# Attention scores whose two products both span 128 partitions, decay ranks with one stationary shape, and later starts for some steps

## The chip, the cores and the metric

The kernel runs on one core of one Trainium2 chip. A core has a matrix engine (TensorE, "PE" in the profile, with its weight loads shown as "PEld"), VectorE ("DVE"), ScalarE ("ACT"), GpSimd ("POOL") and SyncE ("SP"), which here only issues DMA transfers. Each engine works through its own queue in order. The metric is the device time of one execution in microseconds, the median of the runs.

## The reference, cut to what matters

One layer of an encoder on 1024 tokens of width 1024: a half-step feed-forward block with a norm, a mixer with a norm, another half-step feed-forward block with a norm. The mixer projects once, runs neighbourhood attention (8 heads of 64, a window of 8 x 16 on a 16 x 64 grid) and gated linear attention (GLA) in two directions, gates both, and projects out. All in float32.

```python
x <- LN1(alpha*x + 0.5*SwiGLU_1(x))
x <- LN2(alpha*x + W_out(sig(g_na)*P_na(NA(x)) + sig(g_gla)*P_gla(GLA(x))))
x <- LN3(alpha*x + 0.5*SwiGLU_2(x))
# NA, for one row of queries
scores = einsum('bhqd,bhiqjd->bhqij', q_r, k_sel) + bias
p = softmax(scores)
out = einsum('bhqij,bhiqjd->bhqd', p, v_sel)
# GLA, decay of one direction: the decay ranks dec_lr are 16 columns of the projection
log_a = log_sigmoid(dec_lr @ w_dec2 + b_dec) / 16
```

## The kernel before, in words

**Precision.** Matmuls run on a rounded float32 type. A number x is split into a high part xh (x rounded) and a low part xl = x - xh, and a product is the sum of three matmuls: high by high, high by low, low by high. Most filler of PE is such triples of a 128x128 stationary block with 512 moving columns (lines L122 to L124, L559 to L561, L659 to L661, L871 to L873). One triple is one *filler step*; the code counts it as STEP = 0.65 units of its own clock.

**Order.** PE's order is written out by hand. `run` walks through streams of filler steps, adds each step's cost to the clock, and after every step emits the actions whose due time has passed; `at(delay, fn)` queues an action. So an action falls on the first step at or past its due time. The other engines' orders are made by a scheduler from program order and priority.

**Neighbourhood attention.** There are 64 units: 4 head pairs, 2 halves of the rows, 4 blocks of columns, 2 heads. Unit i has, one unit time apart, `na_scores(i)` (two matmuls into one PSUM tile s; then DVE adds the bias and finds the maximum, ACT the exponential, DVE the division), two units later `na_transpose(i)` (three transposes on PE, a copy on ACT), and three units later `na_values` (for two heads at a time, 12 small matmuls). NA_T0 is the due time of unit 0 and NA_DT the distance of units. Filler between them is a projection of V for the GLA (`tok_major`, L871 to L873) and four gates (`gate_gla`, L122 to L124), together 83.2 units of the clock.

**Score operands.** For a pair of heads p, `qk_pair` loads from DRAM, on POOL's queue: for each head the tile q2, which has the high part of that head's q on its own 64 partitions and the low part on the other 64; the tile k2, which has the high part of k on both halves; and one tile kl with the low parts of k of both heads, 64 partitions each. The first score product is q2 by k2 over 128 partitions, (qh + ql) by kh. The second is qh by kl, over the 64 partitions of that head only. `v_block` loads a column block of V for the pair on SP's queue, into a quarter of one tile vp per pair. For pairs 1 to 3, POOL first writes a mark into each new tile, from the small tile of the latest score unit, which holds the loads back to that point.

**Decay ranks.** `decay_rank` multiplies x by 32 columns. Its stationary block of 64 columns has the high part of the weights in columns 0 to 31 and the low part in 32 to 63. By the high part of x all 64 columns are used (L971), by the low part only the first 32 (L967, L970); the two halves of the 64 output rows are added at the end. There are 2 x 16 matmuls of 512 columns.

**Norms.** `Norm` collects eight tiles of 128 features. Its steps are due by lags after each other: lags[0] from the fourth tile to `shift` (L237: a matmul with ones, which gives a provisional mean), lags[1] from the last centring to `stats` (L269: transposes of the sums, then small DVE work), lags[2] to `scale` and lags[3] to `scale2` (L302: matmuls that spread the scales), after which `apply` runs over the eight tiles (two DVE operations, two on ACT, and the low part xl on POOL, L412). LAGS_B is for the second half of the tokens in the first norm, LAGS_2B for the same half in the second norm. The work behind them that needs their result: the fifth token block of `tok_major` (L871 to L873), and the second half of the first gate of the last feed-forward block (L122 to L124).

Of the kernel before, what the change touches and what calls it, by code (L numbers as in the profile page):

```python
# [8 lines left out]
F32 = mybir.dt.float32  # L9
F32R = mybir.dt.float32r  # L10
# [8 lines left out]
P = 128  # L19
D = 1024  # L20
S = 1024
KD = D // P
# [18 lines left out]
GLA_DT = 31.0  # L41
GLA_NEXT = 8.5
GLA_OUT = (15.0, 28.8, 28.8, 35.5)
NA_T0 = 18.0
NA_DT = 0.97
NA_GATES = (4, 5, 6, 7)
GLA_GATES = (1, 2, 3)
FIRST = (1, 2, 4, 8)
STEP = 0.65
LAGS_A = (5.0, 9.5, 8.0, 2.0)  # L50
GAP_A = 1.0
LAGS_B = (2.6, 5.5, 4.7, 1.3)
LAGS_3A = (5.0, 8.0, 9.2, 1.7)
LAGS_3B = (5.0, 7.0, 5.7, 0.2)
GAP_3A = 2.0
GAP_3B = 0.5
LAGS_2A = (7.3, 8.4, 5.6, 2.0)
LAGS_2B = (2.7, 6.1, 3.9, 1.0)
LN_POOL = (1, 2, 3, 5)

COL0 = (0, 8, 24, 40)
COLW = (24, 32, 32, 24)
# [5 lines left out]
def hybrid_layer(ctx, tc, xT, wg1, wu1, wds1, wd1, wg2, wu2, wds2, wd2, wcol, wnv, wgv, wdl, wgate,  # L68
                 wbr, wout, lnp, bias, dec2, bdec, ng, ident_d, masks_d, ln3, outN):
    nc = tc.nc  # L70

    ln_lags = {(0, 0): (LAGS_A, GAP_A), (0, 1): (LAGS_B, 0.0),
               (2, 0): (LAGS_3A, GAP_3A), (2, 1): (LAGS_3B, GAP_3B)}
# [21 lines left out]
    def nm(s):  # L95
        uid[0] += 1
        return f"{s}_{uid[0]}"
# [29 lines left out]
    def dps(shape=(P, HF)):  # L127
        return dense.tile(list(shape), F32, tag="d", name=nm("d"))

    def split(src, hi, lo):  # L130
        nc.scalar.activation(hi, src, AF.Copy)  # L131
        nc.vector.tensor_tensor(lo, src, hi.bitcast(F32), ALU.subtract)  # L132
# [29 lines left out]
    for c1 in FIRST:  # L162
        w = slice(c0 * P, c1 * P)
# [20 lines left out]
    def at(delay, fn):  # L184
        uid[0] += 1
        pending.append((clock[0] + delay, uid[0], fn))
        pending.sort(key=lambda e: e[:2])
# [237 lines left out]
    def stage():  # L425
        return lp.tile([P, HF], F32, tag="sl", name=nm("sl"), bufs=2)
# [391 lines left out]
    x1 = [[None, None] for _ in range(KD)]  # L818
# [22 lines left out]
    qks = dram.tile([4, 4, P, S], F32, tag="qks", name="qks")  # L841
# [114 lines left out]
    def decay_rank():  # L956
        raw = wpool.tile([P, KD, 32], F32, tag="raw", name=nm("raw"), bufs=2)
        nc.sync.dma_start(raw, wdl)
        w = wpool.tile([P, KD, 64], F32R, tag="wh", name=nm("wh"))
        nc.scalar.activation(w[:, :, 0:32], raw, AF.Copy)  # L960
        nc.vector.tensor_tensor(w[:, :, 32:64], raw, w[:, :, 0:32].bitcast(F32), ALU.subtract)
        for h in range(2):
            ps = dps((64, HF))
            for k in range(KD):
                xh, xl = x1[k][h]
                if k:
                    nc.tensor.matmul(ps[0:32], w[:, k - 1, 0:32], x1[k - 1][h][1], start=False,  # L967
                                     stop=False)
                if k == KD - 1:
                    nc.tensor.matmul(ps[0:32], w[:, k, 0:32], xl, start=False, stop=False)  # L970
                nc.tensor.matmul(ps, w[:, k], xh, start=k == 0, stop=k == KD - 1)  # L971
                yield STEP * 2 / 3
            sb = stage()
            nc.scalar.activation(sb[0:32], ps[32:64], AF.Copy)
            nc.vector.tensor_tensor(sb[0:32], sb[0:32], ps[0:32], ALU.add)
            hi, lo = one.tmp(), one.tmp()
            split(sb[0:32], hi[0:32].bitcast(F32R), lo[0:32].bitcast(F32R))
            for i, t in enumerate((hi, lo, hi)):
                nc.sync.dma_start(dls[32 * i:32 * i + 32, h * HF:(h + 1) * HF], t[0:32])
# [18 lines left out]
    npool = pool(nap, "npool")  # L998
    o_na = [[None, None] for _ in range(4)]
    grid = lambda t: t.rearrange("p (r c) -> p r c", c=64)  # L1000
    pair = {}

    def qk_pair(p, mark=None):
        k2 = [npool.tile([P, S], F32R, tag="k2", name=nm("k2"), bufs=4) for _ in range(2)]
        kl = npool.tile([P, S], F32R, tag="kl", name=nm("kl"), bufs=2)
        vp = npool.tile([P, 16, P], F32, tag="vp", name=nm("vp"), bufs=2)
        q2 = [[None, None], [None, None]]
        pair[p] = (q2, k2, kl, vp)
        load = lambda dst, src: nc.gpsimd.dma_start(dst.bitcast(F32), src)
        for h in range(2):  # L1010
            for hh in range(2):
                q2[hh][h] = npool.tile([P, HF], F32R, tag="q2", name=nm("q2"), bufs=8)
        if mark is not None:
            m = mark[:, 0:1]
            for t in (*k2, kl, *q2[0], *q2[1]):
                nc.gpsimd.tensor_copy(t[:, 0:1], m)
        for h in range(2):
            hs = slice(h * HF, (h + 1) * HF)
            for hh in range(2):
                a, o = slice(64 * hh, 64 * hh + 64), slice(64 - 64 * hh, 128 - 64 * hh)  # L1020
                t = q2[hh][h]
                load(t[a], qks[p, 0, a, hs])
                load(t[o], qks[p, 1, a, hs])
                if h == 0:
                    load(k2[hh][a], qks[p, 2, a])
                    load(k2[hh][o], qks[p, 2, a])
            if h == 0:
                load(kl, qks[p, 3])

    def v_block(p, b, mark=None):  # L1030
        vp, w = pair[p][3], COLW[b]
        if mark is not None:
            nc.gpsimd.tensor_copy(vp[:, 4 * b:4 * b + 4, 0:1],
                                  mark[:, 0:1].unsqueeze(2).to_broadcast([P, 4, 1]))
        for g in range(4):
            nc.sync.dma_start(vp[:4 * w, 4 * b + g, :],
                              vgrid[4 * g:4 * g + 4, COL0[b]:COL0[b] + w, p * P:(p + 1) * P])


    na_e, na_t, na_b, na_o, na_mark = {}, {}, {}, {}, {}  # L1040
# [11 lines left out]

    def na_scores(i):
        p, rb, hh, b = na_idx(i)
        q2, k2, kl, vp = pair[p]
        w, c0 = COLW[b], COL0[b]
        nk = 12 * w
        if hh == 0 and b != 2:
            na_b[0] = na_b.pop("next")
            if i < 62:  # L1060
                bias_tile(i + (2 if b != 1 else 4))
        bt = na_b[0]
        a = slice(64 * hh, 64 * hh + 64)
        ka = (slice(4 * rb, 4 * rb + 12), slice(c0, c0 + w))
        qa = slice(P * b, P * b + P)
        s = aux.tile([P, 384], F32, tag="s", name=nm("s"), bufs=2)
        nc.tensor.matmul(s[:, :nk], q2[hh][rb][:, qa], grid(k2[hh])[:, ka[0], ka[1]],
                         start=True, stop=False)
        nc.tensor.matmul(s[:, :nk], q2[hh][rb][a, qa], grid(kl)[a, ka[0], ka[1]],  # L1069
                         start=False, stop=True)  # L1070
        e = npool.tile([P, 384], F32, tag="e", name=nm("e"), bufs=3)
        sm = npool.tile([P, 4], F32, tag="sm", name=nm("sm"), bufs=4)
        nc.vector.tensor_tensor_reduce(e[:, :nk], s[:, :nk], bt[:, hh, :nk], -1.0,
                                       3.0e38, ALU.add, ALU.min, sm[:, 0:1])
        nc.scalar.activation(e[:, :nk], e[:, :nk], AF.Exp, bias=sm[:, 0:1], scale=-1.0,
                             accum_out=sm[:, 1:2])
        nc.vector.reciprocal(sm[:, 2:3], sm[:, 1:2])
        nc.vector.tensor_scalar(e[:, :nk], e[:, :nk], sm[:, 2:3], None, ALU.mult)
        na_e[i] = e
        na_mark[0] = sm  # L1080
# [12 lines left out]
    def na_values(i):  # L1093
        if i % 2 == 0:
            return
        p, rb, hh, b = na_idx(i)
        vp = pair[p][3]
        if i % 8 == 1:
            na_o[0] = aux.tile([P, HF], F32, tag="o", name=nm("po"), bufs=1)
        po = na_o[0]  # L1100
        et = [na_t.pop(i - 1), na_t.pop(i)]
        w = COLW[b]
        for g in range(3):
            for hh in range(2):
                nc.tensor.matmul(po[64 * hh:64 * hh + 64, b * P:(b + 1) * P],  # L1105
                                 vp[:4 * w, 4 * b + rb + g, 64 * hh:64 * hh + 64],
                                 et[hh][:4 * w, g * P:(g + 1) * P], start=g == 0, stop=g == 2)
        if i % 8 == 7:
            hi, lo = atile(F32R), atile(F32R)
            split(po, hi, lo)  # L1110
            o_na[p][rb] = (unblk(hi), unblk(lo))
# [25 lines left out]
    for p in range(1, 4):  # L1137
        t0 = NA_T0 + (16 * p - 10.5) * NA_DT
        at(t0, lambda p=p: qk_pair(p, na_mark[0]))
        for b in range(4):  # L1140
            at(t0 + (1 + 2 * b) * NA_DT, lambda p=p, b=b: v_block(p, b, na_mark[0]))
    na_events(0, 67, NA_T0, NA_T0 + 67 * NA_DT)
    run(tok_major(wgv, lambda t: gv[t], wq=wq), *[gate_gla(j) for j in NA_GATES])
    flush()
# [189 lines left out]
    for hd in range(4):  # L1334
        b = GLA_T0 + GLA_DT * hd
# [70 lines left out]
    for h in range(2):  # L1406
        ln = Norm(HF, 1, LN_EPS, sums, tmp, to_x2(h), LAGS_2B if h else LAGS_2A,
                  0.0 if h else 2.0)
# [102 lines left out]
```

## Time and profile before

| | |
|---|---|
| median of 3 runs | 2116.47 us (2112.81 to 2116.59) |
| the profiled execution | 2112.51 us, of which 2110.7 us span |
| granted clock of PE, mean | 0.995 of full speed |
| instructions in the span | 26717 |
| neighbourhood attention, first score to last values | about 894 to 1072 us |
| decay ranks | 713 to 721 us |
| first norm, second half | statistics at 672 us |
| second norm, second half | shift at 1414 us, statistics at 1442 us |

A row of the timeline has the start and length in us, the engine, the line, the operation, the tiles written and read, the shape (for PE: rows times columns of the array that are used, then partitions times moving columns), the count, and in brackets the idle time before it with what ended it. Lengths of PE's matmuls include the way through the array, so neighbours overlap; the distance of two starts is their pace. A row of a group has busy time and mean ns behind the first bar, idle time behind the second. The table of waits has the total, the number and the longest.

### The profile page before, as it was taken

To read this page: it belongs to the slowest core of one execution; us is meant where nothing else is said; L and a number is where in the kernel's file an instruction comes from. 1 tells how busy PE (TensorE), PEld (TensorE's weight loads), DVE (VectorE), ACT (ScalarE), POOL (GpSimd) and SP (SyncE) were. 2 spreads that over 40 slices of the span, in tenths; PEclk is the share of its full clock that TensorE was granted. 3 is DMA by queue.
4 is the path that set the end of the run, shared out by engine and by line. 5 is a ranking of instruction groups with operands and counts; after the bars stand their busy time and mean duration, and the time that the engine had idled before them with its cause. 6 is when DMAs were issued, how large, how long until landed. Compare 5 with 4: busy or idle time off the path is not lost.

```text
span 2110.7 us, 26717 instructions
## 1 busy us (share of the span) xinstructions
PE 2073.1 (98%) x9722; PEld 1688.4 (80%) x9722; DVE 1379.8 (65%) x2356; ACT 898.4 (43%) x1503; POOL 163.0 (8%) x237
## 2 busy tenths in 40 slices
PE   9999999999999999989999999999999999999997
PEld 7888888888887788766678888877888888888887
DVE  8666776457668964135457774799776776457647
ACT  6444444312234644245565553445544454312222
POOL 0000000000014221212110000034000000000001
PEclk9999999999999999999999999999999999999999
DMA  4444443396630244556444334521343444396622
GB/s 143 148 150 150 158 158 124 130 330 216 221 113 30 88 170 140 153 146 184 147 123 121 110 112 143 176 89 60 118 171 127 175 143 138 122 317 217 240 99 81
DMA packets 156372, 315.59 MB, mean 150 GB/s; under 512 B 17360, under 2 KB 41680, under 8 KB 156240
## 3 DMA queue, kind: packets, MB, share of 16 engines
q1 hardware_dynamic: 136976, 268.26, 37.5%
q0 software_dynamic: 9152, 29.37, 4.7%
q10 hardware_dynamic: 10112, 16.26, 2.5%
q8 instruction: 77, 1.26, 0.2%
q14 instruction: 55, 0.45, 0.1%
HBM read 216.43 MB, written 97.39 MB: 149 GB/s over the span
## 4 chain that ended last, share of the span: by engine, by line
PE 80%; issue 7%; DVE 7%; DMA 3%; ACT 2%; POOL 2%; SPq 0%; ACTq 0%; DVEq 0%; POOLq 0%
PE d L559 16%; PE d L561 16%; PE d L560 16%; PE d L122 5%; PE d L123 5%; PE d L124 5%; PE d L659 3%; PE d L661 3%; PE d L660 3%; PE pt L1087 1%; PE po L1105 1%; PE s L1069 1%; DMA sb<-gts 1%; DMA bt<-in_bias 1%; PE d L871 1%
## 5 line engine op out<-in xcount | busy, mean ns | idle before, releaser
L131 ACT ACTIVATE wh<-raw 128x512 fp32r<-128x512 f32 (+4 forms) x148 | 111.6, 763 | 192.4 <-PE d L560 90.4
L132 DVE TENSOR_TENSOR wl<-raw,wh 128x512 fp32r<-128x512 f32 (+4 forms) x148 | 125.2, 854 | 100.9 <-ACT wh L131 100.9
L122 PE MATMUL d<-xh,wh 128*128 128x512 f32 x384 | 158.4, 413 | 1.0 <-ACT xh L131 0.9
L681 DVE TENSOR_TENSOR a<-a,d 128x512 f32<-128x512 f32 (+1 forms) x152 | 99.9, 657 | 90.9 <-PE d L561 60.5
L559 PE MATMUL d<-a,wh 128*128 128x512 f32 x384 | 149.8, 390 | 2.4 <-DVE hr L587 1.6
L123 PE MATMUL d<-xl,wh 128*128 128x512 f32 x384 | 150.9, 393 | 1.0 <-POOL xl L412 0.5
L124 PE MATMUL d<-xh,wl 128*128 128x512 f32 x384 | 151.1, 394 | 0.0
L561 PE MATMUL d<-xh,wl 128*128 128x512 f32 x384 | 149.5, 389 | 0.5 <-DVE wl L132 0.5
L559 PE MATMUL d<-hh,hh 128*128 128x512 f32 x384 | 149.5, 389 | 0.4 <-ACT hr L923 0.4
L560 PE MATMUL d<-a,wh 128*128 128x512 f32 x384 | 149.4, 389 | 0.0
L559 PE MATMUL d<-xh,wh 128*128 128x512 f32 x384 | 149.4, 389 | 0.0
L560 PE MATMUL d<-xl,wh 128*128 128x512 f32 x384 | 149.4, 389 | 0.0
L561 PE MATMUL d<-a,wl 128*128 128x512 f32 x384 | 149.4, 389 | 0.0
L560 PE MATMUL d<-hl,hh 128*128 128x512 f32 x384 | 149.4, 389 | 0.0
L561 PE MATMUL d<-hh,hl 128*128 128x512 f32 x384 | 149.4, 389 | 0.0
L131 ACT ACTIVATE hh<-sr 128x512 fp32r<-128x512 f32 x168 | 105.6, 631 | 83.7 <-PE d L560 24.4
L659 PE MATMUL d<-hh,wh 128*128 128x512 f32 (+1 forms) x368 | 134.3, 365 | 0.0
L661 PE MATMUL d<-hh,wl 128*128 128x512 f32 (+1 forms) x368 | 133.0, 362 | 0.0
L660 PE MATMUL d<-hl,wh 128*128 128x512 f32 (+1 forms) x368 | 133.0, 361 | 0.0
L132 DVE TENSOR_TENSOR hl<-sr,hh 128x512 fp32r<-128x512 f32 x168 | 114.2, 694 | 1.4 <-ACT hh L131 0.7
L111 ACT ACTIVATE wh<-raw 128x512 fp32r<-128x512 f32 (+1 forms) x77 | 67.5, 877 | 103.6 <-PE d L123 36.9
L131 ACT ACTIVATE oh<-hr 128x512 fp32r<-128x512 f32 x88 | 55.4, 631 | 131.0 <-DVE hr L588 49.0
(335 smaller groups left out, 4928.1 us busy)
## 6 DMA issues: line engine op xcount, KB each, us to landing
raw<-in_wu SPq DMA_DIRECT2D x44, 512.0 KB
raw<-in_wg SPq DMA_DIRECT2D x43, 512.0 KB
ops<-oh SPq DMA_DIRECT2D x84, 256.0 KB
ops<-ol SPq DMA_DIRECT2D x84, 256.0 KB
oh<-ops SPq DMA_DIRECT2D x48, 256.0 KB
ol<-ops SPq DMA_DIRECT2D x48, 256.0 KB
hid<-oh SPq DMA_DIRECT2D x40, 256.0 KB
hid<-ol SPq DMA_DIRECT2D x40, 256.0 KB
```

What stands on the lines that cost most here:

```text
L122: nc.tensor.matmul(ps, a, xh, start=k == 0, stop=False)
L123: nc.tensor.matmul(ps, a, xl, start=False, stop=False)
L124: nc.tensor.matmul(ps, wl[:, k * m:(k + 1) * m], xh, start=False, stop=k == n - 1)
L131: nc.scalar.activation(hi, src, AF.Copy)
L132: nc.vector.tensor_tensor(lo, src, hi.bitcast(F32), ALU.subtract)
L559: nc.tensor.matmul(ps, a, xh, start=first and k == 0, stop=False, **sg)
L560: nc.tensor.matmul(ps, a, xl, start=False, stop=False, **sg)
L561: nc.tensor.matmul(ps, wl[:, k * P:(k + 1) * P], xh, start=False, stop=k == n - 1, **sg)
L659: nc.tensor.matmul(ps, wh, hi, start=k == 0, stop=False)
L660: nc.tensor.matmul(ps, wh, lo, start=False, stop=False)
L661: nc.tensor.matmul(ps, wl, hi, start=False, stop=k == n - 1)
L681: nc.vector.tensor_tensor(a, a, ps, ALU.add)
```

## The change

- The low parts of k get a tile per head, with the same 64 rows on both halves of the partitions, as k2 has them. The second score product is then q2 by kl over all 128 partitions; it also adds the low part of q by the low part of k, which was left out. Each pair has 16 loads on POOL's queue in place of 13, and 8 marks on q and k tiles in place of 7.
- Each column block of V has a tile of its own, from 6 buffers, in place of a quarter of a tile of 2 buffers; blocks 2 and 3 are loaded 9.5 and 11.5 units after the pair's loading is due, in place of 5 and 7.
- Units of attention start at 22.0 in place of 18.0 and stand 0.91 apart in place of 0.97, so that the 67 steps end at 82.97 in place of 82.99.
- In the decay ranks all matmuls use the whole stationary block of 64 columns. Their number stays 16 per half.
- LAGS_B[1] goes from 5.5 to 7.7, LAGS_2B[0] from 2.7 to 5.2 and LAGS_2B[1] from 6.1 to 8.0.

```diff
-NA_T0 = 18.0
-NA_DT = 0.97
+NA_T0 = 22.0
+NA_DT = 0.91
...
-LAGS_B = (2.6, 5.5, 4.7, 1.3)
+LAGS_B = (2.6, 7.7, 4.7, 1.3)
...
-LAGS_2B = (2.7, 6.1, 3.9, 1.0)
+LAGS_2B = (5.2, 8.0, 3.9, 1.0)
...
                 if k:
-                    nc.tensor.matmul(ps[0:32], w[:, k - 1, 0:32], x1[k - 1][h][1], start=False,
-                                     stop=False)
+                    nc.tensor.matmul(ps, w[:, k - 1], x1[k - 1][h][1], start=False, stop=False)
+                nc.tensor.matmul(ps, w[:, k], xh, start=k == 0, stop=False)
                 if k == KD - 1:
-                    nc.tensor.matmul(ps[0:32], w[:, k, 0:32], xl, start=False, stop=False)
-                nc.tensor.matmul(ps, w[:, k], xh, start=k == 0, stop=k == KD - 1)
+                    nc.tensor.matmul(ps, w[:, k], xl, start=False, stop=True)
...
-        kl = npool.tile([P, S], F32R, tag="kl", name=nm("kl"), bufs=2)
-        vp = npool.tile([P, 16, P], F32, tag="vp", name=nm("vp"), bufs=2)
+        kl = [npool.tile([P, S], F32R, tag="kl", name=nm("kl"), bufs=4) for _ in range(2)]
...
-            for t in (*k2, kl, *q2[0], *q2[1]):
+            for t in (*k2, *kl, *q2[0], *q2[1]):
                 nc.gpsimd.tensor_copy(t[:, 0:1], m)
...
                 if h == 0:
-                    load(k2[hh][a], qks[p, 2, a])
-                    load(k2[hh][o], qks[p, 2, a])
-            if h == 0:
-                load(kl, qks[p, 3])
+                    for k, t in ((2, k2[hh]), (3, kl[hh])):
+                        load(t[a], qks[p, k, a])
+                        load(t[o], qks[p, k, a])
...
+        vp = pair[p][3][b] = npool.tile([P, 4, P], F32, tag="vp", name=nm("vp"), bufs=6)
...
-        nc.tensor.matmul(s[:, :nk], q2[hh][rb][a, qa], grid(kl)[a, ka[0], ka[1]],
+        nc.tensor.matmul(s[:, :nk], q2[hh][rb][:, qa], grid(kl[hh])[:, ka[0], ka[1]],
                          start=False, stop=True)
...
-            at(t0 + (1 + 2 * b) * NA_DT, lambda p=p, b=b: v_block(p, b, na_mark[0]))
+            at(t0 + (1, 3, 9.5, 11.5)[b] * NA_DT, lambda p=p, b=b: v_block(p, b, na_mark[0]))
```

More of the change, by code (lines that the diff above doesn't have):

```diff
@@ L1004, in qk_pair @@
         k2 = [npool.tile([P, S], F32R, tag="k2", name=nm("k2"), bufs=4) for _ in range(2)]
-        kl = npool.tile([P, S], F32R, tag="kl", name=nm("kl"), bufs=2)
-        vp = npool.tile([P, 16, P], F32, tag="vp", name=nm("vp"), bufs=2)
+        kl = [npool.tile([P, S], F32R, tag="kl", name=nm("kl"), bufs=4) for _ in range(2)]
         q2 = [[None, None], [None, None]]
-        pair[p] = (q2, k2, kl, vp)
+        pair[p] = (q2, k2, kl, [None] * 4)
         load = lambda dst, src: nc.gpsimd.dma_start(dst.bitcast(F32), src)
@@ L1024, in qk_pair @@
                 if h == 0:
-                    load(k2[hh][a], qks[p, 2, a])
-                    load(k2[hh][o], qks[p, 2, a])
-            if h == 0:
-                load(kl, qks[p, 3])
+                    for k, t in ((2, k2[hh]), (3, kl[hh])):
+                        load(t[a], qks[p, k, a])
+                        load(t[o], qks[p, k, a])
     def v_block(p, b, mark=None):
-        vp, w = pair[p][3], COLW[b]
+        w = COLW[b]
+        vp = pair[p][3][b] = npool.tile([P, 4, P], F32, tag="vp", name=nm("vp"), bufs=6)
         if mark is not None:
-            nc.gpsimd.tensor_copy(vp[:, 4 * b:4 * b + 4, 0:1],
-                                  mark[:, 0:1].unsqueeze(2).to_broadcast([P, 4, 1]))
+            nc.gpsimd.tensor_copy(vp[:, :, 0:1], mark[:, 0:1].unsqueeze(2).to_broadcast([P, 4, 1]))
         for g in range(4):
-            nc.sync.dma_start(vp[:4 * w, 4 * b + g, :],
+            nc.sync.dma_start(vp[:4 * w, g, :],
                               vgrid[4 * g:4 * g + 4, COL0[b]:COL0[b] + w, p * P:(p + 1) * P])
@@ L1054, in na_scores @@
         p, rb, hh, b = na_idx(i)
-        q2, k2, kl, vp = pair[p]
+        q2, k2, kl, _ = pair[p]
         w, c0 = COLW[b], COL0[b]
@@ L1062, in na_scores @@
         bt = na_b[0]
-        a = slice(64 * hh, 64 * hh + 64)
         ka = (slice(4 * rb, 4 * rb + 12), slice(c0, c0 + w))
@@ L1096, in na_values @@
         p, rb, hh, b = na_idx(i)
-        vp = pair[p][3]
         if i % 8 == 1:
@@ L1101, in na_values @@
         et = [na_t.pop(i - 1), na_t.pop(i)]
-        w = COLW[b]
+        w, vp = COLW[b], pair[p][3][b]
         for g in range(3):
@@ L1105, in na_values @@
                 nc.tensor.matmul(po[64 * hh:64 * hh + 64, b * P:(b + 1) * P],
-                                 vp[:4 * w, 4 * b + rb + g, 64 * hh:64 * hh + 64],
+                                 vp[:4 * w, rb + g, 64 * hh:64 * hh + 64],
                                  et[hh][:4 * w, g * P:(g + 1) * P], start=g == 0, stop=g == 2)
```

## The prediction

> **What bounds the kernel now.** I read the page's busy table first, then the windows of the attention stretch, then PE's waits.
>
> ```profile
> PE 2073.1 (98%) x9722; PEld 1688.4 (80%) x9722; DVE 1379.8 (65%) x2356; ACT 898.4 (43%) x1503; POOL 163.0 (8%) x237
> ```
> ```profile
> 909.00:1071.00 162.00, 161.98 (x976) 112.13 (x974) 77.59 (x262) 87.09 (x214) 31.90 (x85) 0.99 0.53 153
> ```
> ```profile
> PE pt L1087 <- DVE e L1078: 5.5, 1, 5.5
> PE s L1069 <- DMA kl<-qks: 3.5, 1, 3.5
> PE pl L269 <- DVE sr L253: 2.1, 1, 2.1
> PE pl L237 <- ACT hr L230: 2.1, 1, 2.1
> ...
> PE pl L269 <- DVE sl L253: 1.7, 1, 1.7
> ```
>
> TensorE (PE) is busy 98% of the span, so only PE time counts, unless the change starves PE. In the attention stretch (the second row: length, then PE, weight loads, DVE, ACT, POOL, clock, DMA share) PE shows no idle time at all, while DVE and ACT are half busy. PE's waits (total, times, longest) name two at the start of attention, 9.0 us together, and three in layer norms, 5.9 us together.
>
> "Busy" is not "at its pace", though. Starts of consecutive matmuls tell the pace:
>
> ```profile
> 1002.17 0.38 PE L1067 MATMUL s<-k,q 128*128 128x288 f32 x1
> 1002.48 0.40 PE L1069 MATMUL s<-kl,q 64*128 64x288 f32 x1
> 1002.80 0.50 PE L122 MATMUL d<-xh,wh 128*128 128x512 f32 x1
> 1003.14 0.40 PE L123 MATMUL d<-xl,wh 128*128 128x512 f32 x1
> ```
> ```profile
> 915.40 0.42 PE L1067 MATMUL s<-k,q 128*128 128x384 f32 x1
> 915.75 0.44 PE L1069 MATMUL s<-kl,q 64*128 64x384 f32 x1
> 916.13 0.50 PE L871 MATMUL d<-wh,xh 128*128 128x512 f32 x1
> ```
> ```profile
> L1069 PE MATMUL s<-kl,q x64: 393/439/686, 897.8 to 1065.3; 64*128 64x288 f32 x32, 64*128 64x384 f32 x32
> ```
> ```profile
> 2071.74 0.28 PE L660 MATMUL d<-hl,wh 128*128 128x256 f32 x1
> ...
> 2073.89 0.28 PE L660 MATMUL d<-hl,wh 128*128 128x256 f32 x1
> ```
> ```profile
> 625.74 0.39 PE L559 MATMUL d<-hh,hr 128*128 128x512 f32 x1
> ...
> 629.60 0.39 PE L661 MATMUL d<-hh,wl 128*128 128x512 f32 x1
> 629.83 1.03 PE L269 MATMUL pl<-ident,sr 128*128 128x128 f32 x8
> 630.62 0.48 PE L659 MATMUL d<-hh,wh 128*128 128x512 f32 x1
> 630.93 0.39 PE L660 MATMUL d<-hl,wh 128*128 128x512 f32 x1
> ```
>
> Where all 128 rows of the array are used throughout, 256 columns take (2073.89 - 2071.74)/18 = 0.119 us and 512 take (629.60 - 625.74)/17 = 0.227 us: 0.42 ns a column. The 64-row product L1069 stands 0.31 us (288 columns) to 0.35 us (384) behind L1067, and the next two steps are 0.32 to 0.38 and, in the first fence, 0.34; there are 32 units of each width. PE loses time on entering and on leaving the 64-row shape; the loss is booked as busy.
>
> **Part 1, the second score product over 128 partitions.** From L1067's start to the second 512-column start behind the pair: 1003.14 - 1002.17 = 0.97 us for 288 columns; for 384 it is 916.13 - 915.40 = 0.73 and the same last step of 0.34, 1.07. Without the switch the same four starts need 288 columns twice (0.12 each with the slope above, call it 0.13) and one of 512 (0.227): 0.49; for 384 (0.173 each), 0.573. One loss stays: behind a run of transposes the first weight load is not hidden, which the rows at 630.62 show for a case with no 64-row shape (0.31 instead of 0.227, so 0.08), and score pairs follow transposes (L1087) in the kernel's order. So 0.57 and 0.65 are left, and the saving is 0.40 and 0.42. I take 0.40 for all 64 units: 64 x 0.40 = **25.6 us**. Bounds: nothing, if the spacing has another cause; 0.97 - 0.49 = 0.48 each, 31 us, if the first load is hidden too. I stay near the middle, since each of its pieces has a row. The matmul count and columns don't change; 128 rows instead of 64 take no longer per column by these rows.
>
> **Part 2, decay ranks with one stationary form.** Before and after, 16 matmuls of 512 columns per half.
>
> ```profile
> 713.14 0.39 PE L971 MATMUL d<-xh,wh 128*64 128x512 f32 x1
> 713.37 0.39 PE L967 MATMUL d<-xl,wh 128*32 128x512 f32 x1
> ...
> 720.28 0.39 PE L971 MATMUL d<-xh,wh 128*64 128x512 f32 x1
> ```
>
> 31 steps between these take 7.14 us, 0.230 each, against 0.227: at most 0.1 us. I cost it at **0**. In the Trainium skill, "TensorEngine Tiling (Array Packing)", section "Tiling Modes" (Key Properties), changing the tiling mode drains the array. The score rows agree with that for 64 against 128 rows; the decay rows don't show it for 32 against 64 columns, where the rule would promise a gain too.
>
> **Part 3, more loading.** Each of four head pairs now loads kl twice as half tiles: 16 POOL loads for 13 and 0.5 MB more. One more POOL mark per pair, 0.18 us, lies beside PE.
>
> ```profile
> 1000.24 0.43 POOL L1016 CAST k<-sm 128x1 fp32r<-128x1 f32 x2 [22.03 <-DVE sm L1073]
> ...
> 1005.38 0.58 POOL L1009 DMA_DIRECT2D kl<-qks  x1
> ```
> ```profile
> kl<-qks POOLq DMA_DIRECT2D x1, 512.0 KB, 7.9
> ```
>
> For pair 3 the last load that a first score needs is issued 5.1 us after the marks and lands 7.9 later (the median row of its DMA list, 997 to 1030), 13 us in all. Pair and loads are 10.5 units apart in the code; the 162 us window above holds some 62 units, 2.6 us each, so the lead is 27 us. Units shrink by 0.40 and by 0.06 of filler (0.97 to 0.91, a filler step of 0.68 us counting 0.65), to about 2.1: lead 22 us. Three more loads in front cost some 1.6 us of issue and 0.5 MB of transfer 2.7 us (below): 13 becomes 17 to 19. **0**, with 3 us of cover left. The value blocks 2 and 3 move from 5 and 7 units behind the pair's loading to 9.5 and 11.5, and are first multiplied 9 units after that, so their SP loads (16 a pair, behind POOL marks) stay covered, and each block has a buffer of its own. Behind a POOL mark stand the pair's loads; behind a value load that waits for its mark stand, on SP, the gate weights (L110). Those are fetched a gate ahead, 16 filler steps at 1.4 a unit, 24 us, so a mark that comes a few units later delays no PE work.
>
> The shorter unit must still hold the softmax chain:
>
> ```profile
> 1004.99 0.49 DVE L1078 TENSOR_SCALAR e<-e,sm 128x288 f32<-128x288 f32 x1
> ```
>
> From the start of L1069 at 1002.48 to the end of this L1078 of the same unit are 3.0 us, then its transposes can run; they stand two units behind, about 4 us. I take 0, at most some 3 us of small waits.
>
> **Part 4, attention starts 4 units later.** Events fall on filler steps of 0.65: 18 is reached after 28 steps, 22 after 34, so 6 more steps (4.1 us) run before the first score, and the sum of filler stays. What holds PE there is ACT, stuck at a store until the loads ebb, before the first exponential:
>
> ```profile
> 903.98 0.60 ACT L876 ACTIVATE sl<-d 128x512 f32<-128x512 f32 x1 [8.66 <-DMA vp<-vscr]
> ```
> ```profile
> q0 software_dynamic: 479, 1.53, 85.4%
> ```
>
> The first row is ACT behind its store of gv; the second is POOL's DMA queue (packets, MB, share of the 16 engines) in 886 to 894: it takes 85% of the engines at 1.53 MB in 8 us, and the 0.52 MB more of pair 0 hold stores and value loads back 2.7 us longer. So the end of the wait moves by 2.7 us and PE has done 4.1 us more by then: **gain 1.4**. Bounds: a loss of 4.6, if one more store waits as long as the 8.66 above; a gain of 9.0, if both waits vanish.
>
> **Part 5, norm steps later.** Each later lag is 3 filler steps of 0.68, 2.0 us; the three waits above (2.1, 2.1, 1.7) are filled with work. But what is late next?
>
> ```profile
> 696.46 0.50 PE L873 MATMUL d<-hh,xl 128*128 128x512 f32 x1 [0.72 <-POOL xl L412]
> ```
> ```profile
> 684.53 11.87 POOL L412 TENSOR_TENSOR xl<-a,xh 128x512 fp32r<-128x512 f32 x8 [6.75 <-ACT xh L411]
> ```
> ```profile
> 1465.47 0.50 PE L123 MATMUL d<-xl,wh 128*128 128x512 f32 x1 [0.50 <-POOL xl L412]
> ```
> ```profile
> 1413.00:1466.00 53.00, 49.27 (x214) 39.44 (x215) 48.34 (x76) 29.33 (x45) 28.39 (x22) 1.00 0.23 80
> ```
>
> In both norms PE already waits at the end for POOL's last xl (eight in a row end at 696.40). Statistics, scales and POOL's run start no earlier: the sums that the waits waited for are DVE's, and DVE is busy 48.3 of 53 us in the second norm. PE reaches 696 and 1465 2 us sooner and waits 2 us longer. **0**, between +1 (steps late by a fraction) and -5.9 (all kept).
>
> **The sum.** 25.6 + 0 + 0 + 1.4 + 0 = 27.0. The profiled execution took 2112.5 (span 2110.7 and 1.8 around it): 2085.5. The three other runs have 2112.8, 2116.5 and 2116.6, median 4.0 above the profiled one; I add half of that: **2087.5**.
>
> **Rivals.**
> - *The column switch drains too*: the decay ranks gain 31 x 0.10 (the entry alone, 0.35 - 0.173 - 0.08), 3.1 us: 2084.4. Against it: the 0.230. The skill's drain rule above is this case. 0.03.
> - *Waits don't come back*: 5.9 of norms and some 3 more at the start: 2079. Against it, the two POOL rows. 0.10.
> - *The start gets worse, small waits in the units*: 4.6 lost for 1.4 gained, 3 us in the chain and 2 of late bias or value tiles: 2087.5 + 6.0 + 5 = 2098.5. For it: POOL's 85% of the DMA engines. 0.14.
> - *It doesn't do what it says*: the spacing stays 0.31 to 0.35, being no matter of rows. Then 2087.5 + 25.6 = 2113. Against it: 128-row matmuls of the same type that add up in one tile show no such gap (the 0.119 and 0.227). It counts as the same, being within 0.2% of the median 2116.5. 0.05.
> - *Slower: the pair loads miss their pair.* Place: first scores of pairs 1 to 3, PE waiting for kl. It decides once loads need over 22 + 10.5 us after the marks (the 27 us gained, plus 4.2, by three); at 34 us each boundary costs 12: 2087.5 + 36 = 2123.5. For it: the POOL queue already fills the engines. Against: 13 us now. 0.04.
>
> **How the numbers follow.** Forecast 0.64. This kernel's runs tell about 0.2% (4.2 us) from no change. Faster: 0.64 + 0.03 + 0.10 + 0.14 = 0.91; same 0.05; slower 0.04. Range 2078 to 2102: it takes in the kept waits below and the worse start above, and leaves out the last two rivals and the corners.
>
> **What would show it.** L1067 to the next start at 0.21 to 0.26 us and no excess behind L1069's successor (else part 1 fell); decay steps still 0.23; no wait at L269 and L237, but waits of 2 us more for xl at L873 and L123; waits at the first scores and transposes of about 8 us in sum; none at later pairs' scores. Many small waits of L1087 for DVE, or any for kl or vp beyond the start, would prove me wrong on cover.

## The result, and the profile after

| | kernel before | changed kernel |
|---|---|---|
| median, four runs each on one chip | 2116.09 us | 2103.91 us |
| lowest and highest | 2112.81, 2116.59 | 2101.69, 2106.27 |
| profiled execution | 2112.5, span 2110.7 | 2106.27, span 2104.4 |

The ratio is 0.9946 (95% interval 0.9929 to 0.9963): 12 us faster, where the sum forecast 27.0 (2087.5 us); 2103.91 lies 1.9 us above the end of the range. The profiled execution of the changed kernel is the slowest of its four and that of the old one is below all of its four, so from trace to trace the gain is only 6.2 us; sums made on the traces go by that figure, comparisons of kernels by medians. Medians and ratios of the runs below leave out two executions at a low granted clock, one of the kernel before (0.654, 2957.38 us) and the profiled one of e3 (0.765, 3760.08 us).

PE's row of the changed kernel's busy table, and the row of its windows for the stretch quoted above (length, PE, weight loads, DVE, ACT, POOL, granted clock, DMA share, GB/s):

```profile
PE 2052.9 (98%) x9722; PEld 1686.4 (80%) x9722; DVE 1381.4 (66%) x2356; ACT 896.6 (43%) x1503; POOL 165.9 (8%) x252
```
```profile
909.00:1071.00 162.00, 147.58 (x999) 115.41 (x1000) 79.91 (x269) 91.45 (x225) 36.19 (x97) 0.95 0.65 175
```

The page still says 98%. The window tells what happened: 162.0 of 162 us busy before, 147.6 now, the clock 0.95 instead of 0.99, and the DMA share 0.65 instead of 0.53. PE's waits over the whole span (total, times, longest):

```profile
PE pt L1083 <- DVE e L1074: 14.5, 4, 13.3
PE pt L1083 <- ACT et L1086: 5.0, 2, 4.0
PE d L123 <- POOL xl L412: 3.1, 4, 1.2
PE d L873 <- POOL xl L412: 2.1, 3, 0.7
PE po L1100 <- ACT et L1086: 1.9, 1, 1.9
...
PE s L1065 <- DMA kl<-qks: 1.7, 1, 1.7
...
PE pl L269 <- DVE sl L253: 1.1, 1, 1.1
```

Attention's waits (pt, po, s) sum to 14.5 + 5.0 + 1.9 + 1.7 = 23.1 us; before they were 9.0. The norms did as forecast: L237 and one L269 are gone, one L269 is down to 1.1, and xl waits of 3.1 and 2.1 stand in their place.

The products themselves, on PE's timeline of the changed kernel:

```profile
933.93 0.42 PE L1063 MATMUL s<-k,q 128*128 128x384 f32 x1
934.20 0.34 PE L1065 MATMUL s<-kl,q 128*128 128x384 f32 x1
934.38 0.39 PE L871 MATMUL d<-wh,xh 128*128 128x512 f32 x1
934.61 0.40 PE L872 MATMUL d<-wl,xh 128*128 128x512 f32 x1
...
1002.45 0.38 PE L1063 MATMUL s<-k,q 128*128 128x288 f32 x1
1002.67 0.29 PE L1065 MATMUL s<-kl,q 128*128 128x288 f32 x1
1002.79 0.39 PE L122 MATMUL d<-xh,wh 128*128 128x512 f32 x1
1003.03 0.40 PE L123 MATMUL d<-xl,wh 128*128 128x512 f32 x1
```

From L1063's start to the second 512-column start it is 0.68 us (384 columns) and 0.58 (288); before, 1.07 and 0.97. That is 0.39 a unit, 25.0 us over 64, as forecast; the medians over the 32 units of each width agree (1.06 to 0.67 and 0.97 to 0.58). Of these, 25.0 - 6.2 = 18.8 us were given back in the two traces. The waits explain 23.1 - 9.0 = 14.1. A part of the other 4.7 is PE's clock after a wait, which the first rows behind the longest one show:

```profile
915.03 0.88 PE L1083 MATMUL pt<-ident,e 128*96 128x128 f32 x3 [13.28 <-DVE e L1074]
...
916.35 0.63 PE L871 MATMUL d<-wh,xh 128*128 128x512 f32 x1
916.77 0.63 PE L872 MATMUL d<-wl,xh 128*128 128x512 f32 x1
```

Starts are 0.42 apart instead of 0.23. The granted clock is 0.61 from 915.03 to 921, 0.76 from 962 to 969 and 0.79 from 1030 to 1038, which makes 5.7 us lost (length times what the clock lacks to 1); the kernel before lost 3.8 in the same way (0.67 from 897.76 to 903, 0.65 from 908.14 to 914). So the clock is about 2 of the 4.7, and where the other 2.8 went stays open.

So what holds PE? The wait names DVE, but DVE waited for ACT. ACT's timeline in the changed kernel (a row with ACTq is a DMA issue in ACT's own order):

```profile
894.68 0.60 ACT L876 ACTIVATE sl<-d 128x512 f32<-128x512 f32 x1 [13.80 <-issue]
906.91 0.33 ACTq L877 DMA_DIRECT2D gv<-sl  x1
907.34 0.60 ACT L876 ACTIVATE sl<-d 128x512 f32<-128x512 f32 x1 [12.06 <-DMA vp<-vscr]
908.57 0.33 ACTq L877 DMA_DIRECT2D gv<-sl  x1
911.47 0.60 ACT L876 ACTIVATE sl<-d 128x512 f32<-128x512 f32 x1 [3.53 <-DMA gv<-sl]
912.10 0.33 ACTq L877 DMA_DIRECT2D gv<-sl  x1
...
913.75 0.53 ACT L1071 ACTIVATE e<-e,sm 128x288 f32<-128x288 f32 x1
...
961.49 1.06 ACT L111 ACTIVATE wh<-raw 128x1024 fp32r<-128x1024 f32 x1 [5.67 <-DMA raw<-in_wgate]
...
1030.79 0.39 ACTq L1046 DMA_DIRECT2D bt<-in_bias  x1
1031.22 0.61 ACT L1071 ACTIVATE e<-e,sm 128x384 f32<-128x384 f32 x1 [3.60 <-DMA vp<-vscr]
```

ACT stands at DMA issues, and at two of these (907.34 and 1031.22) what ends its idle time is the landing of a **value load** (vp), which neither a store of gv nor a bias load touches. The order in the compiled program shows why. A semaphore here is a counter that a DMA raises by 16 when it is done. The bias load issued at 1030.79 has the counter DMAHW5_49, and its issue waits until that stands at 992; it is the first load of a value block (vp_8822), issued by SP, that raises this counter from 976 to 992.

In the compiled program all 985 DMAs of SP and ACT take eight such semaphores in turn, and each issue waits until the earlier DMA on its semaphore is done. So a late value load holds ACT, and every exponential and copy queued behind. The stall at 961.49 is plain lateness: L111 waits for gate weights that SP issues behind 16 value loads. SP's timeline of the changed kernel:

```profile
876.64 32.09 SPq L1033 DMA_DIRECT2D vp<-vscr  x16
```
```profile
937.81 16.84 SPq L1033 DMA_DIRECT2D vp<-vscr  x16
954.75 9.41 SPq L110 DMA_DIRECT2D raw<-in_wgate  x3
```

### The profile page after: what moved, and what is told of

Read it like the earlier page. It is cut to its first block, busy times and chain, and to the rows that moved or that the text cites. A ratio compares the mean times of both kernels' runs of the same rounds, so it can differ in the third digit from the quotient of the medians.

```text
span 2104.4 us, 26747 instructions
## 1 busy us (share of the span) xinstructions
PE 2052.9 (98%) x9722; PEld 1686.4 (80%) x9722; DVE 1381.4 (66%) x2356; ACT 896.6 (43%) x1503; POOL 165.9 (8%) x252
## 4 chain that ended last, share of the span: by engine, by line
PE 79%; issue 7%; DMA 5%; DVE 5%; POOL 2%; ACT 2%; SPq 0%; ACTq 0%; DVEq 0%; POOLq 0%
PE d L559 16%; PE d L561 16%; PE d L560 16%; PE d L122 5%; PE d L124 5%; PE d L123 5%; PE d L661 3%; PE d L660 3%; PE d L659 3%; DMA bt<-in_bias 2%; DMA vp<-vscr 1%; DMA sb<-gts 1%; PE pt L1083 1%; PE po L1100 1%; POOL xl L412 1%
## 5 line engine op out<-in xcount | busy, mean ns | idle before, releaser
L122 PE MATMUL d<-xh,wh 128*128 128x512 f32 x384 | 154.0, 401 | 0.6 <-ACT xh L131 0.5
L559 PE MATMUL d<-xh,wh 128*128 128x512 f32 x384 | 149.4, 389 | 0.0
L112 DVE TENSOR_TENSOR wl<-raw,wh 128x512 fp32r<-128x512 f32 (+1 forms) x77 | 81.1, 1053 | 57.7 <-ACT wh L111 52.0
L111 ACT ACTIVATE wh<-raw 128x512 fp32r<-128x512 f32 (+1 forms) x77 | 67.6, 878 | 107.4 <-PE d L123 37.7
```

Of the source, the lines that this page charges most:

```text
L122: nc.tensor.matmul(ps, a, xh, start=k == 0, stop=False)
L559: nc.tensor.matmul(ps, a, xh, start=first and k == 0, stop=False, **sg)
```

## The experiments

Four theories for the 18.8 us: **A**, the 0.5 MB more a pair keeps other transfers back; **B**, the new times (first score at 22.0, 0.91 a unit) are too late and too dense; **C**, value blocks 2 and 3, loaded later, stand ahead of the gate weights; **D**, ACT's in-order queue is held at its own DMA issues, behind value loads. "Changed" below is 2103.9, from the result above; each run's ratio is to the kernel before on its own chip (2114.7 to 2115.2 there, 2116.09 above, so differences of 1 us mean nothing).

| run | median us | ratio (95% interval) |
|---|---|---|
| e2_zero_half | 2095.58 | 0.9907 (0.9894 to 0.9921) |
| e3_v_early | 2104.74 | 0.9952 (0.9938 to 0.9966) |
| e4_old_times | 2099.74 | 0.9927 (0.9914 to 0.9939) |
| e5_v_pool | 2166.37 | 1.0241 (1.0227 to 1.0255) |
| e6_rest_only | 2112.46 | 0.9989 (0.9980 to 0.9999) |
| e7_sched_only | 2115.97 | 1.0003 (0.9994 to 1.0012) |
| e9_stores_sp | 2102.79 | 0.9941 (0.9929 to 0.9954) |
| e10_bias_sp | 2097.32 | 0.9913 (0.9900 to 0.9927) |
| e11_zero_old | 2099.43 | 0.9927 (0.9915 to 0.9939) |
| e13_v0_later | 2099.88 | 0.9927 (0.9915 to 0.9940) |
| e14_zero_v0 | 2090.66 | 0.9886 (0.9871 to 0.9901) |
| e16_no_v | 2093.59 | 0.9898 (0.9884 to 0.9911) |
| e17_zero_v0_no_v | 2083.38 | 0.9850 (0.9837 to 0.9864) |
| e18_best | 2085.45 | 0.9860 (0.9846 to 0.9873) |
| e19_half_rows | 2117.01 | 1.0015 (1.0006 to 1.0024) |

### Fewer bytes (e2_zero_half)

```diff
-        kl = [npool.tile([P, S], F32R, tag="kl", name=nm("kl"), bufs=4) for _ in range(2)]
+        kl = [klz[p % 2, hh] for hh in range(2)]
...
-                    for k, t in ((2, k2[hh]), (3, kl[hh])):
-                        load(t[a], qks[p, k, a])
-                        load(t[o], qks[p, k, a])
+                    load(k2[hh][a], qks[p, 2, a])
+                    load(k2[hh][o], qks[p, 2, a])
+                    load(kl[hh][a], qks[p, 3, a])
```

(klz holds two pairs of tiles whose other half is set to zero on DVE once.)

> The changed kernel, but the other head's half of each kl tile is zeroed once on DVE and only its own half is loaded: 14 POOL loads and 0.5 MB less a pair, as many bytes as before the change, the same 128-row product (the rows of the other half times zero, so the sum leaves out what the second half of kl adds, as the old kernel did). Theory A (the attention stage gives its gain back because the extra 0.5 MB a pair keeps SP's and ACT's transfers waiting, and ACT with them): 2104 falls to about 2092 to 2096. Theory B (the shorter units and the later start, not the loads): within 3 us of 2104. Theory C (blocks 2 and 3 of the values loaded later, in front of the gate weights): within 3 us of 2104.

Measured 2095.58, 8.3 below the changed kernel: A's number. The bytes count. But PE's waits in the trace are the same kind as before, only shorter (the start's 13.3 became 11.7 and ACT still stands at vp): the bytes set how long, not where.

### Later value blocks (e3_v_early)

```diff
-            at(t0 + (1, 3, 9.5, 11.5)[b] * NA_DT, lambda p=p, b=b: v_block(p, b, na_mark[0]))
+            at(t0 + (1, 3, 6.5, 8.5)[b] * NA_DT, lambda p=p, b=b: v_block(p, b, na_mark[0]))
```

> The changed kernel with value blocks 2 and 3 asked for at 6.5 and 8.5 units behind the pair's loading instead of 9.5 and 11.5, the earliest at which their buffers are free. Theory C (later blocks 2 and 3 stand in SP's queue ahead of the gate weights and hold ACT): some 5 to 9 us faster than the changed kernel, 2095 to 2099, and ACT's wait of 5.67 us for gate weights near 961 goes. Theories A (extra loads) and B (schedule): within 3 us of 2104.

Measured 2104.74, no gain: C falls as far as three units can tell. This rests on the time alone, without a trace.

### The times (e4_old_times, e7_sched_only, e11_zero_old)

```diff
-NA_T0 = 22.0
-NA_DT = 0.91
+NA_T0 = 18.0
+NA_DT = 0.97
```

e4 makes this edit in the changed kernel, e11 in e2's, and e7 its reverse in the old kernel.

> The changed kernel with the first score at 18.0 and 0.97 a unit, as before. Theory B (the units come too fast for a start that lies too late): 2092 to 2097, the stage at PE's pace but for the start. Theories A and C: within 3 us of 2104, since the loads and their order are the same; the wait at the first transposes stays near 13 us.

> The old kernel with the first score at 22.0 and 0.91 a unit, and nothing else. Theory B (the new times themselves cost): slower by 3 to 8 us, 2118 to 2123. The prediction had 1.4 gained at the start, 2114. Theory A (only with more bytes to load): within 2 us of 2115.

> Both cures at once: the other head's half of each kl tile zeroed once and not loaded, and the first score at 18.0 and 0.97 a unit. If extra loads and new times cost independently, 8.3 and 4.2 below 2104: 2091 to 2092. If both only move one and the same wait (ACT behind the value loads), no better than the better of the two: 2095 to 2098.

e4 gave 2099.74, 4.2 below the changed kernel: part of B's 7 to 12, not all. e7 gave 2115.97, about 1 us from the kernel before: with the old product the new times cost nothing that can be measured, though its trace has a start of 10.5 us where the old one had 5.5 and 3.5. So B by itself falls. e11 gave 2099.43: under the old times fewer bytes gain nothing (0.3), under the new ones 8.3. The cures do not add up. In the middle of the stage ACT's timeline has three long stalls in each, 2.2, 2.4 and 4.7 us in e4 and 4.1, 5.0 and 2.9 in e11; why fewer bytes don't shorten them there, these runs leave open.

### The rest alone (e6_rest_only)

The old kernel with the change's decay order and LAGS_B and LAGS_2B, nothing else.

> The old kernel with the decay order and the two norm lags of the change, and nothing of the attention part. The prediction had 0 for these two: within 2 us of the old kernel's 2115. Rival: what the decay order (0.9 us, seen behind the decay ranks) and the norms give is kept, 2 to 6 us faster.

Measured 2112.46, ratio 0.9989: about 2.5 us faster on medians, with an interval that almost touches 1 (0.2 to 4.2 us). The size is not settled; from trace to trace there is no gain (span 2111.2 against 2110.7). It is no loss to speak of, and too small to matter for the 18.8.

### Who waits in which queue (e5_v_pool, e9_stores_sp, e10_bias_sp)

```diff
-            nc.sync.dma_start(vp[:4 * w, g, :],
+            nc.gpsimd.dma_start(vp[:4 * w, g, :],
```

> The changed kernel with the 64 value loads issued by POOL behind the pair's loads, not by SP. ACT's and SP's DMA issues share eight completion semaphores in turn, so in the changed kernel a bias load or a store on ACT waits for an SP value load that took the same semaphore before; here they have no value loads among them. Theory D (ACT's queue, and the softmax behind it, is held by those waits): faster by 8 to 18 us, 2086 to 2096, no ACT wait for vp left. Theory A (bytes on the way, whoever issues them): within 4 us of 2104, with the waits on PE as long as now, put down to another load; if POOL's 16 more issues a pair come too late, slower, 2110 or more, with PE waiting at the value products for vp.

Measured 2166.37: D's number missed by 70 us. What came true is the side case named under A, slower with PE waiting at the value products for vp, and that is a matter of POOL's issue, which says nothing on A or D. POOL's timeline of this run:

```profile
963.90 0.69 POOL L1033 DMA_DIRECT2D vp<-vscr  x1 [2.76 <-issue]
...
970.20 0.68 POOL L1033 DMA_DIRECT2D vp<-vscr  x1 [2.38 <-issue]
```

Here one value load leaves POOL every (970.20 - 963.90)/2 = 3.2 us, and this pair's 16 take from 948.17 to 990.49, 42 us; PE's waits name vp at the value products, 20.2 us in ten, and POOL itself became the bound.

Next the other way round, ACT's issues to SP: e9 moves the stores, e10 the stores and the bias loads.

```diff
-            nc.scalar.dma_start(dst(t), sb)
+            (eng or nc.scalar).dma_start(dst(t), sb)
...
-            nc.scalar.dma_start(gts[j, :, h * HF:(h + 1) * HF], sb)
+            nc.sync.dma_start(gts[j, :, h * HF:(h + 1) * HF], sb)
...
-        nc.scalar.dma_start(bt[:, :, :nk], bias[p, rb, :, 2 * BOFF[b]:2 * BOFF[b] + 2 * nk]
+        nc.sync.dma_start(bt[:, :, :nk], bias[p, rb, :, 2 * BOFF[b]:2 * BOFF[b] + 2 * nk]
```

> The changed kernel with the stores of gv and gts issued by SP instead of ACT; every load as it is. Theory D (ACT's in-order queue is held at its own stores, which wait for a completion semaphore that an SP value load took, and the softmax behind them waits): the 13 us ahead of the first transposes shrink by 4 to 9 us and so does the time, 2095 to 2100. Theory A alone (bytes on the way hold back what the softmax itself reads, the bias and the value tiles): within 2 us of 2104.

Measured 2102.79, which is no gain beyond the noise. ACT in e9 shows that I had the start half wrong:

```profile
911.35 1.21 ACT L876 ACTIVATE sl<-d 128x512 f32<-128x512 f32 x2 [17.90 <-DMA gv<-sl]
```

ACT now waits for a free stage buffer (sl), whose store stands on SP behind the 16 value loads: the same cause by another wire. And the loads of dec2, behind the gts stores on SP, came late for PE after the stage, 2.5 us in its waits.

> The changed kernel with bias loads, gv and gts stores all issued by SP, so ACT issues no DMA in the stage. Theory D without more: no ACT stall for DMA in the middle of the stage, as good as without the value loads there, but the loads of dec2 and dlT behind the gts stores cost 4 us after the stage as they did when SP took the stores alone: 2094 to 2100. Rival: SP's order is the bottleneck whoever waits in it; the bias comes behind 16 value loads (17 us to issue) and DVE and PE wait for it instead: 2106 or more.

Measured 2097.32, inside D's range. ACT's stalls at bias and store issues are gone from its timeline; behind the start it has two over 2 us, one for gate weights (2.69) and one for DVE (2.25, at 980.18). PE's waits from 909 on in this run:

```profile
PE pt L1083 <- DVE e L1074: 11.8, 2, 11.5
PE pt L1083 <- ACT et L1086: 1.9, 1, 1.9
...
PE pt L1083 <- DVE sm L1073: 0.7, 1, 0.7
```

The start's 11.5 stays; the middle, with 0.6 more at po, is down from 8.1 to 3.5. One bias seems to come late behind other issues of SP: DVE begins on it at 979.62, though both score products had ended by 977.67, and SP had issued that bias at 976.19. It costs PE little, and the time is far below the rival's 2106, so the rival falls.

### Without the value loads, and with the first ones later (e16_no_v, e13_v0_later, e14_zero_v0)

e16 returns pair 0's tile for the later pairs; e13 asks for three of pair 0's blocks behind the first scores; e14 is e13's edit on top of e2's.

```diff
+        if p:
+            pair[p][3][b] = pair[0][3][b]
+            return
```
```diff
-    for b in range(4):
-        v_block(0, b)
+    v_block(0, 0)
+    for b in range(1, 4):
+        at(NA_T0 + (2 * b - 1) * NA_DT, lambda b=b: v_block(0, b, na_mark[0]))
```

> The changed kernel without the value loads of pairs 1 to 3: their value products read pair 0's values (this leaves 48 of the 64 loads out and makes the outputs wrong). POOL's loads, all marks but those of the values, bias, stores and gate weights stay. Theory D (ACT's own DMA issues wait for completion semaphores that value loads hold): ACT's stalls in the middle of the stage near 952, 961, 996 and 1031 go, and with them 8.0 us of PE waits and 2 to 3 of cold clock behind them: 2093 to 2096; the 13 us at the start stay. Theory A (POOL's extra bytes by themselves keep bias and gate weights back): the stalls stay, 2101 to 2105.

Measured 2093.59, inside D's range: 10.3 below the changed kernel with every POOL byte still there. PE's waits in the stage of this run:

```profile
PE pt L1086 <- DVE e L1077: 14.7, 5, 13.2
...
PE s L1068 <- DMA kl<-qks: 1.0, 1, 1.0
```

The start's 13.2 is untouched and the middle's 8 us are down to 1.5. So value loads are what holds ACT there; with them gone, POOL's extra bytes alone hold next to nothing. Whether it is their place in the order or their own bytes this run can't tell; e10, which keeps every byte and moves only ACT's issues, speaks for the order.

> The changed kernel with pair 0's value blocks 1, 2 and 3 asked for 1, 3 and 5 units into the attention, behind a mark, instead of ahead of it. Theory D: the four gv stores ahead of the first exponential no longer wait for 16 value loads, ACT comes to the first exponential at about 903 to 906 instead of 913.8, and 6 to 9 us are gained at the start: 2095 to 2098. Rival: the blocks come late for the first value products, or their loads hold ACT some units later, and what is gained at 915 is lost by 940: 2101 to 2106.

Measured 2099.88: 4.0 gained, between the two expectations. ACT's timeline of this run:

```profile
905.25 0.54 ACT L1071 ACTIVATE e<-e,sm 128x288 f32<-128x288 f32 x1
...
945.63 0.60 ACT L131 ACTIVATE a<-po 128x512 fp32r<-128x512 f32 x1 [3.72 <-DMA vp<-vscr]
...
954.61 1.06 ACT L111 ACTIVATE wh<-raw 128x1024 fp32r<-128x1024 f32 x1 [5.48 <-DMA raw<-in_wgate]
```

The first exponential comes at 905.25 instead of 913.75, as D has it, and PE's wait there falls from 13.3 to 6.0. But a stage that runs ahead of its loads meets the next ones sooner: the stall at 945 is 3.72 where the changed kernel had 1.38.

> Zeroed halves (0.5 MB less a pair) and pair 0's value blocks 1 to 3 behind the first scores, with the times of the change. If the start and the bytes add up: 6 to 9 us below the 2095.6 of the zeroed halves alone, 2087 to 2090, near what was forecast for the change. If the start only moves its wait into the next units: 2093 to 2097.

Measured 2090.66: 4.9 below e2, between the two expectations; as in e13, part of what the start gives is lost later.

### The whole account (e17_zero_v0_no_v, e18_best, e19_half_rows)

e17 is e14 with e16's edit. e18 is e14 with bias loads and gv stores on SP, gts stores left on ACT. e19 is the changed kernel with the old product on the new tiles:

```diff
-        nc.tensor.matmul(s[:, :nk], q2[hh][rb][:, qa], grid(kl[hh])[:, ka[0], ka[1]],
+        nc.tensor.matmul(s[:, :nk], q2[hh][rb][a, qa], grid(kl[hh])[a, ka[0], ka[1]],
```

> Zeroed halves, pair 0's value blocks 1 to 3 behind the first scores, and no value loads of pairs 1 to 3 (their value products read pair 0's values: 48 loads left out, outputs wrong). If start, value loads and bytes are the whole account: the 8 us of waits left in the version with both cures shrink to the 5 at the start, 2083 to 2088, and 28 us or more below the kernel before. If something else takes part of the 25 us: 2089 to 2091, as with the value loads.

> The whole computation with zeroed halves, pair 0's value blocks 1 to 3 behind the first scores, and bias loads and gv stores issued by SP (gts stores stay on ACT). If ACT's own issues are what is left: 2084 to 2088. If the bias behind SP's value loads comes late instead: 2091 to 2096.

Measured 2083.38 and 2085.45, both inside the first range given: 31.3 and 29.2 us below the kernel before. e17's attention waits in the trace are 5.9 us. PE's attention waits in e18, whose product, like the old kernel's, leaves out what the other 64 rows of kl add:

```profile
PE pt L1092 <- DVE sm L1082: 3.3, 1, 3.3
PE pt L1092 <- DVE e L1083: 3.1, 3, 1.8
...
PE po L1109 <- ACT et L1095: 1.1, 1, 1.1
```

7.5 us, less than the old kernel's 9.0. The 3.3 is a bias that came late behind SP's value loads (DVE waits 2.5 us for it), the second case of the expectation in small. 25.0 for the product, 1.5 for these and what e6 gives (2.5, of uncertain size) make 29.0. The clock is not in this sum, so that it comes so near to 29.2 is in part luck. Start, value loads and bytes together account for what was given back; the share of each is not shown, since the cures do not add up. e18, the best version of the whole kernel found, is faster than both.

> The changed kernel with the old product: over the 64 rows of its own head, from the kl tiles as they are now loaded (this leaves out what the other 64 rows add). The cost of the switch alone: 64 x 0.39 = 25 us more PE time. If the stalls of ACT stay as long under the longer unit: 2104 + 25 = 2129. If the longer unit covers most of them, as the old kernel's did: 2116 to 2121, and the gain given back belongs to the shorter unit as much as to the loads.

Measured 2117.01: the lower range. In the changed surroundings the new product is worth 2117.0 - 2103.9 = 13 us, not 25. PE's attention waits in e19:

```profile
PE pt L1084 <- DVE e L1075: 14.2, 3, 13.3
...
PE pt L1084 <- ACT et L1087: 1.9, 1, 1.9
```

The start's 13.3 is the same as in the changed kernel, but the waits in the middle are 2.8 us where the changed kernel has 8.1, though the traced execution of e19 (2121.06 us) is the slowest of its eleven. With 0.39 us more in each unit, ACT comes later to its casts and issues, and more of the loads that it is held by have landed: of the changed kernel's four stalls of ACT for DMAs in the middle (5.67, 3.60, 1.90 and 1.38 us) two are left, of 0.63 us and this one:

```profile
964.87 1.06 ACT L111 ACTIVATE wh<-raw 128x1024 fp32r<-128x1024 f32 x1 [4.15 <-DMA raw<-in_wgate]
```

All that the change does beside the product costs about 2 us under the old product (2117.0 against 2114.7; 1 to 5 by the interval) and about 13 under the new one (25.0 - 12.2).

## Why the prediction was wrong

**Right, part 1.** 25.0 us measured on the matmul starts, 25.6 forecast. It is the 64-row product that takes this time: in e19, with that product put back and nothing else, the four starts stand 1007.24 - 1006.17 = 1.07 us apart again.

```profile
1006.17 0.42 PE L1064 MATMUL s<-k,q 128*128 128x384 f32 x1
...
1007.24 0.40 PE L123 MATMUL d<-xl,wh 128*128 128x512 f32 x1
```

And e18 shows that the gain can be had in time.

**Right, part 2.** The decay's column switch costs nothing: PE's timeline of the changed kernel has the steps at (720.25 - 713.12)/31 = 0.230 us, the same as before, with one 64-column form throughout.

```profile
713.12 0.40 PE L968 MATMUL d<-xh,wh 128*64 128x512 f32 x1
...
720.25 0.39 PE L970 MATMUL d<-xl,wh 128*64 128x512 f32 x1
```

The drain rule in the Trainium skill, "TensorEngine Tiling (Array Packing)", section "Tiling Modes", agrees with the 0.39 a unit for rows and not with these columns.

**Wrong, part 3: "0, with 3 us of cover left".** The cover was worked out for PE's own inputs, and these came in time: no later pair's score waited for kl. Left out was who else waits. The sentence on SP says that a late mark "delays no PE work", because the gate weights are fetched a gate ahead; but ACT casts them (L111) in the order in which it does the softmax, and stood 5.67 us. And no sentence asked what ACT's own issues wait for. The trace of before shows such a wait at the start, in its row at 903.98, quoted in part 4, where ACT is held 8.66 us behind a store until vp lands. I read it as a matter of the start only. In the middle that trace gave no warning. These are all of ACT's waits for DMAs in the kernel before, from 860 to 1075:

```profile
ACT sl L876 <- DMA q<-qks: 13.4, 1, 13.4
ACT sl L876 <- DMA vp<-vscr: 8.7, 1, 8.7
...
ACT L1075 <- DMA vp<-vscr: 1.0, 1, 1.0
```

All three end by 905.6. From 909 to 1071 ACT never idles for more than 1.73 us, and then for PE: the loads landed before ACT came to them. The stalls arose with the change. Cost in the trace: 8.1 us of waits in the middle (23.1 less the start's 13.3 and 1.7), and some of the lower clock behind them.

**Wrong, part 4: "gain 1.4".** The start's waits went from 9.0 to 15.0 us (13.3 and 1.7), 6 lost, outside even the bound of 4.6. The step that failed is "the end of the wait moves by 2.7 us": the first exponential moved from 906.85 to 913.75, by 6.9. It comes at 909.01 in e4, the changed kernel with the old times, and at 912.51 in e7, the old kernel with the new times. So the change without its times makes 2.2, close to the forecast, and the times without the rest 5.7; they overlap, so the two don't sum to 6.9. With six more filler steps ahead of the first score, one more evict and store of gv (the pair at 911.47 and 912.10) stands on ACT ahead of the first exponential. The evict waits 3.53 us for an earlier store, and the stores wait for value loads, whose issue now ends at 908.7 (876.64 + 32.09) and ended at 905.4 before. The lower bound named the mechanism; I took the other value. e13 tells the size: the value loads are 7 of the 13.3.

**Right, part 5, as far as the traces tell.** The norm waits came back at xl: 5.2 us in sum, where there were 1.2 and the three waits of 5.9, of which 1.1 are left. On medians e6, which has parts 2 and 5, leaves up to 4 us of gain open.

**The rivals.** "The start gets worse, small waits in the units" is what happened, at 0.14. Its 11 us were too few: it had 4.6 lost at the start (6.0 measured), and 5 in the units (8.1 and the clock). None of the terms allowed for what e19 shows, that a gain of 25 us of PE time in a stage brings ACT to its casts and issues before the loads that hold them have landed. In the old kernel PE, busy in 161.98 of 162 us, set a pace at which the loads kept ahead; I took that for ACT having room.

## What to carry to other kernels

When a bound engine gets faster in a stage, the engines that feed it come sooner to everything they wait for. Go through their loads, and the DMA issues in their queues, and ask of each how long ahead of its use it lands in the trace of before; neither busy shares (ACT at half) nor the idle times of that trace show it. An engine that computes and also issues DMAs can be held by any transfer that its issue is ordered behind, also one whose data it never touches; keep issues off the engine that feeds the bound one, or keep slow loads out of its turn. Fewer bytes (e2, 8.3 us), later loads (e13, 4.0) and SP's queue for ACT's issues (e10, 6.6) did not add up; together they gave 29.2 us, a little more than the forecast gain. A queue can also be the wrong one: POOL's cost 62 us (e5).

## What was not expected of the hardware

Small loads against POOL's queue. The DMA view of the changed kernel in 886 to 894, then in 904 to 912, when POOL's queue is empty (queue, packets, MB, share of the 16 engines):

```profile
q0 software_dynamic: 444, 1.41, 79.4%
...
q1 hardware_dynamic: 90, 0.05, 3.6%
```
```profile
q1 hardware_dynamic: 1190, 0.59, 26.6%
```

SP's value loads (q1) move 0.05 MB in 8 us beside POOL's, and 0.59 MB without: they nearly stop. Of pair 0's 16 value loads, 0.9 MB (8 of 64 KB and 8 of 48), about 0.2 MB moves between 880 and 902, by the DMA view of each two microseconds; the rest follows when POOL's last load has landed, at 903. ACT's stores, which wait for value loads, are late with them.

The Trainium skill, "DMA: Bandwidth & Descriptors", section "Queues, rings and completion order", says that each DMA engine goes round the queues that have work for it, a packet of descriptors at a time. These rows show that such a turn is no protection by bytes or by count: 90 packets of the profile against 444. Whether a packet of the profile is one in that sense, and what sets the ratio, no run here shows.
